# Two neighbouring rows per partition for the expert down weights, and a Silu that writes even and odd columns apart

## The chip, the cores and the metric

The kernel runs on one core of a Trainium2 chip. A core has TensorE (matrix multiplication; in the profile PE, its weight loads PEld), VectorE (DVE), ScalarE (ACT), GpSimd (POOL) and SyncE (SP), which issues the DMAs, and 16 DMA engines that move data between device memory and the on-chip memory SBUF. Matmuls write to PSUM. The metric is device time in microseconds (us); less is better.

## The reference

A trunk of two decoder layers, 256 tokens of width 1024, all in float32. Each layer has attention and a state-space mixer side by side, then a channel mixer: a dense SwiGLU in layer 0, and in layer 1 a mixture of eight experts of which each token takes two. Only the experts matter here:

```
def swiglu(h, w_gate, w_up, w_down):
    return (jax.nn.silu(h @ w_gate) * (h @ w_up)) @ w_down

logits = (hf @ router_w).astype(jnp.float32)
top_val, top_idx = lax.top_k(logits, TOP_K)          # TOP_K = 2 of 8
gates = jax.nn.softmax(top_val, axis=-1)
# per expert e: rows of its tokens -> swiglu(x, w_gate[e], w_up[e], w_down[e]) * gate, added to the token
```

An expert has w_gate and w_up of 1024 x 3584 and w_down of 3584 x 1024. The down projection sums over the 3584 columns of silu(gate) * up: in which order they are summed is free, as long as a column of the product meets its own row of w_down.

## The kernel before, in words

**Weights as a stream.** All weights pass once through SBUF as units of 1 MB, [128 partitions x 2048 floats]. `Stream` keeps their order: SyncE issues the load of a unit as soon as a buffer is free (eight `raw` buffers, and `slot` buffers lent by other tiles when those are done; line 124 is the DMA). A `slot` can be two or four smaller tiles; such a load is issued in pieces.

**Two kinds of experts.** The experts are taken in an order found at run time and alternate between two kinds, "H" and "L". An H expert has up to 128 token rows. Its weights are split in two parts that TensorE multiplies fast, `hi` (ScalarE, L157) and `lo` (VectorE, L158), two halves of 1024 floats per unit, and each product takes three matmuls (L698, L699, L700; L699 is the one that needs `lo`). An L expert has 64 rows and is multiplied in plain float32 from the raw tile (gate and up L1524, down L1546), both halves of TensorE's columns at once.

**Chunks.** Each expert goes through its 3584 columns in chunks of 1024, 1024, 1024 and 512. For a chunk the kernel makes gate (`g`) and up (`u`) in PSUM, then Silu of `g` to SBUF on ScalarE (L1672) and the product with `u` on VectorE (L1673), both named `sg`, 128 x 512 each: an H chunk of 1024 columns has two, an H chunk of 512 or an L chunk one (the L form of the last chunk has 256 columns per half). Then `sg` is transposed in blocks of 128 columns (L1575 for H, L1533 for L), and the transposed blocks are multiplied with the down weights into `ps_d` and `ps_a` (H) or `ps_m` (L). A down unit is 256 rows of w_down, two blocks of 128 rows, one for each of two neighbouring transposed blocks. Chunks of an H and an L expert take turns, and the down matmuls of a chunk run after gate and up of the next.

**What sets the order.** The order on each engine is fixed when the program is built, by a scheduler that follows the program's data; on the chip each engine works through its list and waits for semaphores. VectorE's list has `sg` products and `lo` splits in one row, ScalarE's has Silus and `hi` splits.

The change touches `add_m` (lines 344 to 353), which describes the loads of expert weights, and the loop of the expert stage in `moe` (lines 1659 to 1675). In `add_m` the source of a unit is

```
.rearrange("(k p) f -> p k f", p=P)
```

so that partition p gets row p of each block of 128 rows: two pieces of 4 KB, 512 KB apart in device memory, for a down unit.

Of the kernel before, what the change touches and what calls it, by code (L numbers as in the profile page):

```python
# [11 lines left out]
AF = mybir.ActivationFunctionType  # L12
OP = mybir.AluOpType
AX = mybir.AxisListType

P = 128
# [203 lines left out]
def trunk(ctx, tc, x, c, positions, ada_w, ada_b, norm_mix_g, norm_ffn_g, w_in, w_out, attn_sinks,  # L220
# [3 lines left out]
    V, A, G, PE = nc.vector, nc.scalar, nc.gpsimd, nc.tensor  # L224
# [7 lines left out]
    def ps(tag):  # L232
        return psum.tile([P, 512], F32, name="ps_" + tag, tag=tag, bufs={"w": 3, "m": 3, "d": 1, "a": 1}[tag])
# [110 lines left out]
    def add_m(tag, w4d, p, r0, rows, c0, width):  # L344
        def loads():
            e = expert_at[p]
            if isinstance(e, int):
                src = w4d[0, e, r0:r0 + rows, c0:c0 + width].rearrange("(k p) f -> p k f", p=P)
            else:
                src = w4d[0, bass.ds(e, 1), r0:r0 + rows, c0:c0 + width].rearrange("e (k p) f -> p (e k) f", p=P)  # L350
            return [(0, 2048, src)]

        units.append(dict(kind="w" if kinds[p] == "H" else "m", tag=(tag, p), loads=loads, n=2048))
# [12 lines left out]
    for p, ch in items:  # L366
# [4 lines left out]
        rows = 2048 // width * P  # L371
# [60 lines left out]
    p = ps("w")  # L432
# [29 lines left out]
    for b in range(2):  # L462
        for h in range(2):
            p = ps("w")
# [896 lines left out]
    def moe(route):  # L1361
# [20 lines left out]
        for b in range(2):  # L1382
            V.max_index(ix[:, b, :], mx[:, b, :], lo8[:, b, :])
        V.tensor_tensor(oh8, iota8[:, None, None, :].to_broadcast([P, 2, 2, NE]), ix[:, :, 0:2, None].to_broadcast([P, 2, 2, NE]),
                        op=OP.is_equal)
# [52 lines left out]
        wide = act.tile([P, 4, NE, NE], F32, name="sort", tag="sq", bufs=3)  # L1438
# [66 lines left out]
        def gather(ps_, oh):  # L1505
            return [lambda k2=k2: gather_part(ps_, oh, k2) for k2 in range(4)] + [lambda: info(ps_, oh)]
# [5 lines left out]
        def step_pend():  # L1512
            if pend:
                pend.pop(0)()
# [14 lines left out]
        def transpl(sg, width):  # L1529
            nm = width // 2 // P  # L1530
            p_ = ps("m")
            for m_ in range(nm):
                PE.transpose(p_[:, m_ * P:(m_ + 1) * P], sg[:, m_ * P:(m_ + 1) * P], ident)  # L1533
            ht = act.tile([P, nm, 2, half], F32, name="ht", tag="mt", bufs=2)
            A.activation(ht.rearrange("p m c s -> p (m c s)"), p_[:, 0:nm * P], AF.Copy)
            return ht

        def downl(p, ch, y, ht):
            c0, width = chunks[ch]
            nm = width // 2 // P  # L1540
            for u in range(width // 256):
                j = S.take_m(("d", p))
                for t_ in range(2):
                    ft = u * 2 + t_
                    for c_ in range(2):
                        PE.matmul(y[half * c_:half * (c_ + 1), :], ht[:, ft % nm, ft // nm, :],  # L1546
                                  S.col(j, t_ * D + c_ * 512, t_ * D + (c_ + 1) * 512), start=(ch == 0 and ft == 0),
                                  stop=(c0 + (ft + 1) * P == ED), skip_group_check=True)
                S.release(j)
# [20 lines left out]
        def transp(sgs):  # L1570
            out_ = []
            for sg in sgs:
                p_ = ps("m")
                for j in range(4):
                    PE.transpose(p_[:, j * P:(j + 1) * P], sg[:, j * P:(j + 1) * P], ident)  # L1575
                hh = act.tile([P, 4, P], F32R, name="hh", tag="mt", bufs=2)
                hl = act.tile([P, 4, P], F32R, name="hl", tag="pt", bufs=2)
                pv = p_.rearrange("p (j s) -> p j s", j=4)
                with tc.issue_after(S.last_hi):
                    A.activation(hh, pv, AF.Copy)  # L1580
                with tc.issue_after(S.last_lo):
                    V.tensor_tensor(hl, pv, hh.bitcast(F32), op=OP.subtract)  # L1582
                out_.append((hh, hl))
            return out_

        def down(p, ch, y, hs):
            for u in range(chunks[ch][1] // 256):
                w = S.take(("d", p), 2)
                for k in range(2):
                    ft = u * 2 + k  # L1590
                    hh, hl = hs[ft // 4]
                    for n_ in range(2):
                        mm3(y[n_], hh[:, ft % 4, :], hl[:, ft % 4, :], w.hi(k, n_ * 512, (n_ + 1) * 512),
                            w.lo(k, n_ * 512, (n_ + 1) * 512), ch == 0 and ft == 0, chunks[ch][0] + (ft + 1) * P == ED)
                    S.used()

        def combine(e, y):
# [10 lines left out]
            def piece(m2):  # L1608
                p_ = ps("m")
                for k in range(2):  # L1610
                    m_ = m2 * 2 + k
                    c0 = m_ % 4 * P
                    i, rows = (m_ // 4, slice(0, P)) if kinds[e] == "H" else (0, slice(m_ // 4 * half, (m_ // 4 + 1) * half))
                    PE.matmul(p_[:, k * T:(k + 1) * T], yh[i][rows, c0:c0 + P], oht[rows], start=True, stop=False)
                    PE.matmul(p_[:, k * T:(k + 1) * T], yl[i][rows, c0:c0 + P], oht[rows], start=False, stop=True)
                for k in range(2):
                    m_ = m2 * 2 + k
                    V.scalar_tensor_tensor(xT[:, m_, :], p_[:, k * T:(k + 1) * T], mod(1, 5)[:, m_:m_ + 1], xT[:, m_, :],
                                           op0=OP.mult, op1=OP.add)
            return [lambda m2=m2: piece(m2) for m2 in range(4)]  # L1620

        def flip(t):
            sg_, p, ch = t
            if kinds[p] == "H":
                hs = transp(sg_)
                return lambda y: down(p, ch, y, hs)
            ht = transpl(sg_[0], chunks[ch][1])
            return lambda y: downl(p, ch, y[0], ht)
# [3 lines left out]
        for p, ch in items:  # L1632
            kind = kinds[p]
            width = chunks[ch][1]
            final = (p, ch) == items[-1]
            if (p, ch) == (4, 0):
                flip(prev)(y[prev[1]])
                while pend:
                    step_pend()
                pend.extend(combine(prev[1], y[prev[1]]))  # L1640
                prev = None
                while pend:
                    step_pend()
                overflow(cnt_i, late_slot, gfull, htok_h, htok_l)
                S.lend(first_moe + LATE_LIMIT, lambda: [act.tile([P, D], F32, name="slot", tag=t) for t in ("cx", "qr")])
                S.lend(first_moe + ROWS_LIMIT, lambda: [act.tile([P, 2 * D], F32, name="slot", tag="xbc")])
            if final:
                while pend:
                    step_pend()
                fin = prefinish(p, inf)  # L1650
            nb = width // 512 if kind == "H" else 1
            g = [ps("w") for _ in range(nb)]
            if kind == "H":
                proj("g", p, g, gather((0,), oh0) if (p, ch) == (0, 0) else ())
            else:
                projl("g", p, width, g[0])
            if prev is not None:
                step = flip(prev)
            u = [ps(t) for t in ("w", "m")[:nb]]
            if kind == "H":  # L1660
                proj("u", p, u)
            else:
                projl("u", p, width, u[0])
                S.prime(LOOK + 2)
            ahead = together.get((p, ch))
            if ahead:
                oh = onehot(ahead)
            wide = 512 if kind == "H" else width // 2
            sg = []
            for g_, u_ in zip(g, u):  # L1670
                s_ = act.tile([P, 512], F32, name="sg", tag="rm", bufs=2)
                A.activation(s_[:, 0:wide], g_[:, 0:wide], AF.Silu)  # L1672
                V.tensor_tensor(s_[:, 0:wide], s_[:, 0:wide], u_[:, 0:wide], op=OP.mult)  # L1673
                sg.append(s_)
            if final:
                for b in range(2):
                    xbank(1, b, fin[3])
                tail = flip((sg, p, ch))
            if ahead:
                for f in gather(ahead, oh):  # L1680
                    f()
            if prev is not None:
                step(y[prev[1]])
                if prev[2] == LAST:
                    while pend:
                        step_pend()
                    pend.extend(combine(prev[1], y[prev[1]]))
            if ch == 0:
                y[p] = (ps("d"), ps("a")) if kind == "H" else (ps("m"),)
            prev = (sg, p, ch)  # L1690
# [134 lines left out]
```

## Time and profile before

| | |
|---|---|
| median of 3 runs | 1399.41 us (1398.51 to 1399.52) |
| the profiled execution, its own time | 1397.93 us |
| its span in the profile | 1395.8 us |
| TensorE busy | 1321.7 us, 95% |
| VectorE busy | 857.9 us, 61% |
| ScalarE busy | 643.7 us, 46% |
| main DMA queue | 466.72 MB in 155616 packets |

The profile is of one execution. A row of a timeline has the start and the duration in microseconds, the engine, the line, what is written <- what is read, the shape, and in brackets the idle time of the engine before it with what ended that. Matmuls are pipelined: one that lasts 0.40 us can be followed by the next after 0.23 us. A row of waits gives the waiting engine, tile and line, what it waited for, the total in us, how often, and the longest. A busy engine is not a limit by itself, and idle time of an engine that nobody waits for costs nothing.

### The profile page before, as it was taken

To read this page: it belongs to the slowest core of one execution; us is meant where nothing else is said; L and a number is where in the kernel's file an instruction comes from. 1 tells how busy PE (TensorE), PEld (TensorE's weight loads), DVE (VectorE), ACT (ScalarE), POOL (GpSimd) and SP (SyncE) were. 2 spreads that over 40 slices of the span, in tenths; PEclk is the share of its full clock that TensorE was granted. 3 is DMA by queue.
4 is the path that set the end of the run, shared out by engine and by line. 5 is a ranking of instruction groups with operands and counts; after the bars stand their busy time and mean duration, and the time that the engine had idled before them with its cause. 6 is when DMAs were issued, how large, how long until landed. Compare 5 with 4: busy or idle time off the path is not lost. (4 is left out here: it accounts for less than half of the span.)

```text
span 1395.8 us, 20220 instructions
## 1 busy us (share of the span) xinstructions
PE 1321.7 (95%) x7642; PEld 953.8 (68%) x7642; DVE 857.9 (61%) x1297; ACT 643.7 (46%) x923; POOL 20.1 (1%) x22
## 2 busy tenths in 40 slices
PE   6999999999899979999999999987999999999996
PEld 3788699999798868666464756656557467756643
DVE  5587598778689579556254744546537348845532
ACT  3456454444465547445143543533536236744412
POOL 0020000000020010000000000000000000000000
PEclk9999999999999989999999999997999999999998
DMA  9963799999434549899999999989999999999993
GB/s 324 349 237 109 277 388 363 325 348 340 159 127 146 197 149 340 333 406 400 402 409 409 409 409 409 398 349 400 363 409 409 402 401 409 409 379 409 402 402 127
DMA packets 158214, 468.77 MB, mean 336 GB/s; under 512 B 10560, under 2 KB 39456, under 8 KB 155040
## 3 DMA queue, kind: packets, MB, share of 16 engines
q1 hardware_dynamic: 155616, 466.72, 87.8%
q8 instruction: 61, 1.00, 0.3%
q10 hardware_dynamic: 2496, 0.72, 0.2%
q14 instruction: 41, 0.34, 0.1%
HBM read 466.36 MB, written 1.05 MB: 335 GB/s over the span
## 5 line engine op out<-in xcount | busy, mean ns | idle before, releaser
L158 DVE TENSOR_TENSOR lo<-raw,hi 128x1024 fp32r<-128x1024 f32 (+1 forms) x346 | 413.4, 1226 | 98.5 <-ACT hi L157 95.3
L157 ACT ACTIVATE hi<-raw 128x1024 fp32r<-128x1024 f32 (+1 forms) x346 | 354.9, 1057 | 220.7 <-PE ps_m L699 69.2
L699 PE MATMUL ps_w<-lo,xh 128*128 128x512 f32 x352 | 141.1, 401 | 0.7 <-DVE lo L158 0.7
L700 PE MATMUL ps_w<-hi,xh 128*128 128x512 f32 x352 | 140.3, 400 | 0.2 <-DVE xh L1503 0.2
L698 PE MATMUL ps_w<-hi,xh 128*128 128x512 f32 x352 | 133.8, 404 | 6.9 <-PEq L1246 5.6
L158 DVE TENSOR_TENSOR lo<-slot,hi 128x1024 fp32r<-128x1024 f32 (+1 forms) x112 | 128.0, 1181 | 15.7 <-ACT hi L157 15.7
L157 ACT ACTIVATE hi<-slot 128x1024 fp32r<-128x1024 f32 (+1 forms) x112 | 111.6, 1026 | 33.2 <-PE ps_w L700 25.7
L1673 DVE TENSOR_TENSOR sg<-sg,ps_w 128x512 f32<-128x512 f32 (+1 forms) x32 | 20.9, 654 | 171.6 <-PE ps_w L1524 129.8
L1524 PE MATMUL ps_w<-raw,xl 128*64 128x512 f32 (+1 forms) x624 | 125.7, 545 | 0.0
L698 PE MATMUL ps_m<-act_hi,hi 128*128 128x256 f32 (+1 forms) x368 | 104.6, 285 | 7.6 <-ACT hi L157 4.7
L700 PE MATMUL ps_m<-act_hi,lo 128*128 128x256 f32 (+1 forms) x368 | 104.1, 284 | 0.4 <-DVE lo L158 0.4
L699 PE MATMUL ps_m<-act_lo,hi 128*128 128x256 f32 (+1 forms) x368 | 104.2, 284 | 0.0
L1524 PEld LDWEIGHTS ps_w<-raw,xl 128*64 128x64 f32 x624 | 43.9, 137 | 72.2 <-issue 65.7
L1580 ACT ACTIVATE hh<-ps_m 128x512 fp32r<-128x512 f32 x28 | 16.2, 595 | 154.9 <-PE ps_m L1575 131.8
L698 PEld LDWEIGHTS ps_w<-hi,xh 128*128 128x128 f32 x352 | 67.3, 192 | 23.5 <-issue 5.9
L1524 PE MATMUL ps_w<-slot,xl 128*64 128x512 f32 (+1 forms) x400 | 81.4, 536 | 0.0
L699 PEld LDWEIGHTS ps_w<-lo,xh 128*128 128x128 f32 x352 | 67.4, 191 | 17.7 <-DVE lo L158 1.9
L700 PEld LDWEIGHTS ps_w<-hi,xh 128*128 128x128 f32 x352 | 67.0, 191 | 16.4 <-DVE xh L1503 0.7
L1546 PE MATMUL ps_m<-raw,ht 128*64 128x512 f32 x328 | 76.6, 599 | 0.0
L698 PEld LDWEIGHTS ps_m<-act_hi,hi 128*128 128x128 f32 (+1 forms) x368 | 68.1, 185 | 11.5 <-ACT hi L157 5.2
L1582 DVE TENSOR_TENSOR hl<-ps_m,hh 128x512 fp32r<-128x512 f32 x28 | 18.8, 688 | 92.8 <-ACT hh L1580 92.8
L1672 ACT ACTIVATE sg<-ps_w 128x512 f32<-128x512 f32 (+1 forms) x44 | 24.9, 576 | 102.5 <-PE ps_w L1524 76.6
(428 smaller groups left out, 2484.3 us busy)
## 6 DMA issues: line engine op xcount, KB each, us to landing
raw<-in_moe_w_down SPq DMA_DIRECT2D x84, 1024.0 KB, 13.5
raw<-in_moe_w_gate SPq DMA_DIRECT2D x79, 1024.0 KB, 12.4
raw<-in_moe_w_up SPq DMA_DIRECT2D x61, 1024.0 KB, 12.6
raw<-in_ada_w SPq DMA_DIRECT2D x40, 1024.0 KB, 7.2
slot<-in_moe_w_up SPq DMA_DIRECT2D x25, 1024.0 KB, 14.0
slot<-in_moe_w_gate SPq DMA_DIRECT2D x48, 512.0 KB, 12.7
slot<-in_moe_w_up SPq DMA_DIRECT2D x46, 512.0 KB, 13.8
slot<-in_moe_w_down SPq DMA_DIRECT2D x20, 1024.0 KB, 13.7
```

Of the source, the lines that this page charges most:

```text
L157: self.last_hi = nc.scalar.activation(hi[:, o:o + w], t, AF.Copy).ins
L158: self.last_lo = nc.vector.tensor_tensor(lo[:, o:o + w], t, hi[:, o:o + w].bitcast(F32), op=OP.subtract).ins
L698: PE.matmul(o_, s_hi, m_hi, start=start, stop=False, skip_group_check=True)
L699: PE.matmul(o_, s_hi, m_lo, start=False, stop=False, skip_group_check=True)
L700: PE.matmul(o_, s_lo, m_hi, start=False, stop=stop, skip_group_check=True)
L1524: PE.matmul(b[half * c_:half * (c_ + 1), 0:wide], xl[:, kk_, :], S.col(j, o_, o_ + wide), start=(kk_ == 0), stop=(kk_ == KT - 1), skip_gro ...
L1546: PE.matmul(y[half * c_:half * (c_ + 1), :], ht[:, ft % nm, ft // nm, :], S.col(j, t_ * D + c_ * 512, t_ * D + (c_ + 1) * 512), start=(ch ...
L1580: A.activation(hh, pv, AF.Copy)
L1582: V.tensor_tensor(hl, pv, hh.bitcast(F32), op=OP.subtract)
L1672: A.activation(s_[:, 0:wide], g_[:, 0:wide], AF.Silu)
L1673: V.tensor_tensor(s_[:, 0:wide], s_[:, 0:wide], u_[:, 0:wide], op=OP.mult)
```

## The change

Three edits. A down unit's load gives each partition two neighbouring rows of w_down: partition p gets rows 2p and 2p+1 of the 256, which lie one behind the other in device memory, so that a whole-tile load has packets of 8 KB. The two matmul blocks of a unit are then its even and its odd rows. To match, Silu and the product write `sg` with the even columns of each 256 in one block of 128 and the odd in the next; they read `g` and `u` in order. `in_pairs` is the view of `sg` for that: u counts groups of 256 columns, q the pairs in it, k even or odd, and k runs fastest. The transposes, the matmuls and all other loads are the same. Loads into lent buffers of two or four small tiles keep pieces of 4 or 2 KB.

```
@@ add_m
         def loads():
             e = expert_at[p]
+            if tag == "d":
+                pick_e = w4d[0, e:e + 1] if isinstance(e, int) else w4d[0, bass.ds(e, 1)]
+                return [(0, 2048, pick_e[:, r0:r0 + rows, :].rearrange("e (p k) f -> p (e k f)", p=P))]
             if isinstance(e, int):
                 src = w4d[0, e, r0:r0 + rows, c0:c0 + width].rearrange("(k p) f -> p k f", p=P)
@@ moe
+        def in_pairs(t, w):
+            return t[:, 0:w].rearrange("p (u k q) -> p u q k", k=2, q=P)
+
...
                 s_ = act.tile([P, 512], F32, name="sg", tag="rm", bufs=2)
-                A.activation(s_[:, 0:wide], g_[:, 0:wide], AF.Silu)
-                V.tensor_tensor(s_[:, 0:wide], s_[:, 0:wide], u_[:, 0:wide], op=OP.mult)
+                sv = in_pairs(s_, wide)
+                A.activation(sv, g_[:, 0:wide].rearrange("p (u q k) -> p u q k", k=2, q=P), AF.Silu)
+                V.tensor_tensor(sv, sv, u_[:, 0:wide].rearrange("p (u q k) -> p u q k", k=2, q=P), op=OP.mult)
                 sg.append(s_)
```

## Rows read from the trace of the kernel before

**Rows 1.** The page: span, and busy time of TensorE

```profile
span 1395.8 us, 20220 instructions
...
PE 1321.7 (95%) x7642; PEld 953.8 (68%) x7642; DVE 857.9 (61%) x1297; ACT 643.7 (46%) x923; POOL 20.1 (1%) x22
```

**Rows 2.** Windows: stretch, busy us by engine, TensorE's granted clock, DMA share, GB/s

```profile
core 0: us, PE busy (x) PEld busy (x) DVE busy (x) ACT busy (x) POOL busy (x), PEclk, DMA share, GB/s
560.00:1365.00 805.00, 778.52 (x3637) 486.05 (x3635) 431.17 (x475) 354.05 (x418) 0.00 (x0) 0.99 1.01 397
...
770.00:805.00 35.00, 35.00 (x155) 25.51 (x155) 24.34 (x26) 19.85 (x22) 0.00 (x0) 1.00 1.03 409
...
1130.00:1137.00 7.00, 7.00 (x34) 3.48 (x34) 0.76 (x2) 0.00 (x0) 0.00 (x0) 1.00 1.05 387
```

**Rows 3.** Waits of TensorE in 560 to 1365 us, longest in total first

```profile
PE ps_m L1533 <- DVE sg L1673: 6.9, 8, 0.9
PE ps_w L698 <- PEq L1246: 5.6, 1, 5.6
PE ps_m L1614 <- DVE oht L1606: 4.3, 1, 4.3
PE ps_d L699 <- DVE lo L158: 2.7, 2, 1.3
PE ps_m L1614 <- ACT yh L1603: 1.6, 2, 0.8
PE ps_m L1614 <- DVE xT L1618: 1.3, 2, 0.7
```

**Rows 4.** Timelines of ScalarE, VectorE and TensorE, 1340 to 1349 us

```profile
1340.83 2.00 ACT L157 ACTIVATE hi<-slot 128x1024 fp32r<-128x1024 f32 x2 [0.84 <-DMA slot<-in_moe_w_down]
...
1346.33 0.69 DVE L1673 TENSOR_TENSOR sg<-sg,ps_w 128x512 f32<-128x512 f32 x1 [15.22 <-PE ps_w L1524]
1346.93 1.22 DVE L158 TENSOR_TENSOR lo<-slot,hi 128x1024 fp32r<-128x1024 f32 x1
...
1348.20 0.50 PE L699 MATMUL ps_d<-lo,hh 128*128 128x512 f32 x1 [1.33 <-DVE lo L158]
```

**Rows 5.** Timelines of VectorE and TensorE, 1050 to 1054 us

```profile
1051.29 0.69 DVE L1673 TENSOR_TENSOR sg<-sg,ps_w 128x512 f32<-128x512 f32 x1 [12.48 <-PE ps_w L1524]
1051.89 1.22 DVE L158 TENSOR_TENSOR lo<-slot,hi 128x1024 fp32r<-128x1024 f32 x1
...
1052.03 0.66 PE L1533 MATMUL ps_m<-ident,sg 128*128 128x128 f32 x4 [0.86 <-DVE sg L1673]
...
1053.17 0.50 PE L699 MATMUL ps_d<-lo,hh 128*128 128x512 f32 x1
```

**Rows 6.** Lines by form: count | busy us, mean ns of one | idle before

```profile
L1673 DVE TENSOR_TENSOR sg<-sg,ps_w 128x512 f32<-128x512 f32 x28 | 19.2, 687 | 158.0 <-PE ps_w L1524 123.8 <-PE ps_w L700 34.2
...
L1673 DVE TENSOR_TENSOR sg<-sg,ps_w 128x256 f32<-128x256 f32 x4 | 1.7, 421 | 13.6 <-issue 7.7 <-PE ps_w L1524 5.9
...
L1333 DVE TENSOR_REDUCE shw<-shw 128x8 f32<-128x64 f32 x1 | 0.3, 262 | 0.0
...
L1445 DVE TENSOR_REDUCE keys<-sort 128x8 f32<-128x64 f32 x1 | 0.2, 220 | 0.0
...
L1448 DVE TENSOR_REDUCE keys<-sort 128x8 f32<-128x64 f32 x1 | 0.2, 214 | 0.0
...
L1672 ACT ACTIVATE sg<-ps_w 128x512 f32<-128x512 f32 x40 | 23.4, 595 | 85.5 <-PE ps_w L1524 59.6 <-PE ps_w L700 25.5
...
L1672 ACT ACTIVATE sg<-ps_w 128x256 f32<-128x256 f32 x4 | 1.5, 384 | 17.0 <-PE ps_w L1524 17.0
```

**Rows 7.** Timelines of ScalarE, VectorE and TensorE, 1017 to 1021 us

```profile
1017.79 0.60 ACT L1672 ACTIVATE sg<-ps_w 128x512 f32<-128x512 f32 x1
1018.29 1.05 ACT L157 ACTIVATE hi<-raw 128x1024 fp32r<-128x1024 f32 x1
...
1019.37 1.23 DVE L158 TENSOR_TENSOR lo<-raw,hi 128x1024 fp32r<-128x1024 f32 x1 [3.24 <-ACT hi L157]
...
1020.86 0.39 PE L699 MATMUL ps_w<-lo,xh 128*128 128x512 f32 x1
```

**Rows 8.** DMA issues of down weights: count, KB each, median us to landing

```profile
raw<-in_moe_w_down SPq DMA_DIRECT2D x84, 1024.0 KB, 13.5
...
slot<-in_moe_w_down SPq DMA_DIRECT2D x20, 1024.0 KB, 13.7
```

## The prediction

> **What bounds the kernel now.** I read the page first. TensorE is busy for 1321.7 of 1395.8 us [rows 1], which alone settles nothing, because the expert stage (from about 560 us to 1365 us) keeps the DMA engines as busy. So I took the windows of that stage next [rows 2]. Over 805 us TensorE is busy 778.5 us, and the DMA engines show a share of 1.01 at 397 GB/s. In a typical 35 us piece both columns are full, 35.00 us of TensorE and 1.03 of DMA at 409 GB/s. Which one waits for the other has to come from the waits. The idle time of TensorE in the stage is 805.0 - 778.5 = 26.5 us, and its eleven rows of waits account for 26.3 us of it; the six largest are shown [rows 3]. The reader is to see that no row names a DMA. The largest, 6.9 us in eight pieces, is a wait for the VectorE product `sg` (L1673); 2.7 us in two pieces is a wait for `lo` (L158).
>
> Then I looked at a place where weights are late. At 1340.83 ScalarE starts its split of a down weight after waiting 0.84 us for a DMA [rows 4]. TensorE does not feel it: the second half of the split, `lo`, stands on VectorE behind `sg`, which needs the end of the up projection and runs only at 1346.33. So `lo` starts at 1346.93, over six microseconds after the DMA landed. TensorE paces the stage, transfers run at their cap a little ahead of it, and the exposed holes are the places where VectorE's `sg` is in front.
>
> **The change, part by part.** No instruction is added, removed or moved: every engine's list stands in the same order with the same count. Two things differ: the shape of 104 DMAs, and the address pattern of 44 Silus (L1672) and 44 products (L1673).
>
> *The DMAs.* 84 + 20 whole-tile down loads [rows 8] get one packet of 8 KB for two of 4 KB. At 409 GB/s over 16 engines a 4 KB packet holds its engine 16 x 4096 / 409 = 160.2 ns; in a stretch where the narrow chunk's 2 KB packets are on the wire the rate is 387 GB/s [rows 2], 84.7 ns for 2 KB. The second 2 KB of a packet cost 75.5 ns, so 9.2 ns of each packet are fixed. Two 4 KB packets (320.4 ns) become one of 311.2 ns. A 1 MB load saves 8 such pairs per engine, 74 ns, and 104 loads save 7.7 us of DMA time. That is what it would be worth on the path. I take 0: TensorE's own work covers it, as no wait of TensorE in the stage ends with a DMA [rows 3]. What the faster loads do is land a little earlier. If that cover were gone, the price is the 7.7 us.
>
> *The product `sg`.* It reads the Silu from SBUF and writes back to SBUF with the pair index innermost, so that successive elements lie 128 elements (512 bytes) apart; `u` is still read in order from PSUM. Today the 512-wide form takes 687 ns and the 256-wide 421 ns, 1.04 ns per element [rows 6]. The trace has no such write, and of reads with a far inner step one clean case: the reduction L1333 reads 64 elements at a step of 32 bytes and takes 262 ns, where L1445 and L1448 reduce 64 neighbouring elements in 220 and 214 ns [rows 6]. That is 45 ns more for 64 elements, 0.70 ns each. Applied to 512 elements it is +0.36 us. The lower end is 0, since the engine may take any address at one element a cycle; a gain I exclude, as the same elements pass. The upper end is one more cycle per element, 512 x 1.04 = +0.53 us. I take +0.36, from the nearest row.
>
> [...]
>
> How often is it exposed? Between 1050 and 1053 [rows 5] TensorE ends the up projection of a half-width expert, `sg` starts at 1051.29 and ends at 1051.98, and the transpose L1533 starts at 1052.03, after 0.86 us of idle TensorE. Nothing is between them, so what `sg` grows by, TensorE waits longer; behind `sg` on VectorE stands `lo`, ending at 1053.11, and the matmul L699 that needs it starts at 1053.17, so it shifts by the same amount. This pattern occurs 8 times (the 8 pieces of 6.9 us), and the pattern of rows 4, with L699 waiting for `lo` behind `sg`, twice. That is 10 exposed products of 512 elements: 10 x 0.36 = 3.6 us (0 to 5.3 us). The other 34 have their transposes further away, behind down matmuls or the next projection, and I take them at nothing.
>
> *The Silu.* Its reads stay in order, its writes get the same step. It takes 595 ns for 512 elements and 384 ns for 256, 0.82 ns per element [rows 6]. No row has a far-stepped ScalarE write: the bounds are 0 and one more of these, +0.42 us. In the half-width experts it runs under the up projection. In the full-width experts two Silus stand in ScalarE's queue ahead of the `hi` split for the next weights [rows 7]: the second starts at 1017.79, `hi` at 1018.29, `lo` ends at 1020.60 and the matmul that needs it starts at 1020.86, a slack of 0.26 us. Four chunks look like this, and a fifth has one Silu and hardly any slack. At the upper end the price is 4 x (0.84 - 0.26) + 0.36 = 2.7 us. I take 0, because the one row on which I price a far step is a read.
>
> **Sum.** The profiled execution took 1397.93 us, its span of 1395.8 us and 2.1 us around it. 0 for the DMAs, 0 for the Silus, +3.6 us for the products: 1401.5 us. The median of the runs is 1399.41 us, 1.5 us above that execution, so the prediction is 1403.0 us.
>
> **Rivals.** *Free address pattern.* If the engines take the pattern at full rate, nothing on the path changes: 1399.4 us, and the change costs as little as it gives. For it speaks that only one small reduction shows a price; against it, that this reduction is undisturbed and dearer by a fifth.
>
> *Transfers decide.* If the stage really runs at the pace of the loads, the 7.7 us come out: 1399.4 - 7.7 = 1391.7 us, and anything over 2.8 us of it already counts as faster. For it: a DMA share of 1.03 at a flat 409 GB/s [rows 2], and ScalarE waiting for down weights [rows 4]. Against it: 26.3 of 26.5 us of TensorE's idle time have other names. It decides from the point where loads land later than `sg` ends. [...] The rows of TensorE's waits do not show it here.
>
> *Both engines pay a full cycle per element.* 5.3 us for products and 2.7 us for Silus: 1407.4 us.
>
> *8 KB packets move worse than 4 KB ones.* If a load took 5% longer (0.13 us, 104 times), 13 us of DMA time would use up the lead that rows 4 show to be short, and I would expect some 4 us of new waits: about 1403 us, slower for another reason. Nothing in the rows speaks for it.
>
> **How the numbers follow.** A change under 0.2% (2.8 us) cannot be told from none. Forecast (products pay, Silus hidden) 0.38; both pay in full 0.12; worse packets 0.03; free pattern 0.37; transfers decide 0.10. That gives slower 0.53, same 0.37, faster 0.10. The range reaches from just under the free case to near the full price, 1398.4 to 1406.6 us; the forecast's own is 1401.5 to 1405.0.
>
> **What would show it.** L1673's successor at 512 elements should take about 1.05 us (687 ns if the pattern is free, 1.22 us at a full cycle), and TensorE's wait for it should grow from 6.9 to about 9.8 us in eight pieces, with the one for `lo` from 2.7 to 3.4 us. Silu should stay near 595 ns, or else `hi` and `lo` after it come late and L699 gets waits with full-width experts. GB/s in windows of down loads should rise from 409 towards 420 with no gain in time. The prediction is wrong if the product's duration stays put, if a wait of TensorE for a DMA disappears that I did not see, or if the expert stage shortens by microseconds.

## The result, and the profile after

The changed kernel takes 1406.17 us in the median of 6 runs (1404.38 to 1407.81), the kernel before 1398.76 us in 6 runs beside them (1398.31 to 1399.52). The ratio is 1.0051, with a 95% interval from 1.0041 to 1.0062: slower by some 7 us. The forecast of slower holds, but its price, 3.6 us, is half of what came: the time stands just inside the wide range (to 1406.6 us) and above the forecast's own (1401.5 to 1405.0 us). The profiled execution took 1406.9 us, with a span 9.0 us longer than before.

The page of the changed kernel, with the packets, bytes and share of the main DMA queue in its last row, answers to [rows 1] and to the table ahead:

```profile
span 1404.8 us, 20226 instructions
...
PE 1322.7 (94%) x7642; PEld 954.0 (68%) x7642; DVE 871.5 (62%) x1297; ACT 659.5 (47%) x923; POOL 20.1 (1%) x22
...
q1 hardware_dynamic: 142304, 466.72, 86.9%
```

TensorE does the same work (1322.7 us against 1321.7). VectorE has 13.6 us more, ScalarE 15.8. The same bytes went in 13312 fewer packets, which is 104 loads of 128 pairs made into one.

The windows of the expert stage, with the columns of [rows 2], and the DMA issues of down weights, which answer to [rows 8]:

```profile
560.00:1375.00 815.00, 783.58 (x3654) 488.57 (x3655) 444.95 (x481) 369.28 (x420) 0.00 (x0) 0.99 1.00 395
770.00:805.00 35.00, 35.00 (x152) 27.38 (x152) 28.70 (x29) 21.15 (x22) 0.00 (x0) 1.00 1.02 413
```

```profile
raw<-in_moe_w_down SPq DMA_DIRECT2D x84, 1024.0 KB, 11.7
...
slot<-in_moe_w_down SPq DMA_DIRECT2D x20, 1024.0 KB, 11.0
```

In the shorter window the rate went from 409 to 413 GB/s, and a load lands 1.8 to 2.7 us earlier after its issue. TensorE is full there as before; whether the loads matter at all is left to the first experiment.

The lines by form of the two operations (L1679 is the Silu, L1680 the product), which answer to [rows 6]:

```profile
L1679 ACT ACTIVATE sg<-ps_w 128x512 f32<-128x512 f32 x40 | 43.0, 1111 | 85.2 <-PE ps_w L1527 59.7 <-PE ps_w L703 25.5
L1680 DVE TENSOR_TENSOR sg<-sg,ps_w 128x512 f32<-128x512 f32 x28 | 30.4, 1084 | 154.8 <-PE ps_w L1527 123.4 <-PE ps_w L703 31.4
```

The product grew from 687 to 1084 ns, +0.40 us; +0.36 was forecast. The Silu grew from 595 to 1111 ns, +0.52 us, which is more than the upper bound of 0.42 that I had set.

The waits of TensorE between 560 and 1375 us, and below them those between 545 and 570 us, which answer to [rows 3]:

```profile
PE ps_m L1536 <- DVE sg L1680: 9.9, 8, 1.2
PE ps_w L701 <- PEq L1249: 5.0, 1, 5.0
PE ps_m L1617 <- DVE oht L1609: 4.3, 1, 4.3
PE ps_d L702 <- DVE lo L158: 3.3, 2, 1.6
PE ps_w L702 <- DVE lo L158: 2.5, 7, 0.7
```

```profile
PE ps_m L1497 <- DVE sg L1680: 0.7, 1, 0.7
```

One row of before from 560 to 1365 us, which [rows 3] leave out, belongs beside them:

```profile
PE ps_w L699 <- DVE lo L158: 0.7, 1, 0.7
```

The wait of the transposes for `sg` grew from 6.9 to 9.9 us in the same eight pieces, and the wait for `lo` behind `sg` from 2.7 to 3.3 us in two. Both are as forecast (9.8 and 3.4). Two waits were not forecast. In the projections TensorE waits seven times for `lo`, 2.5 us, where before it was 0.7 us once. And before the gather of the next experts (L1497) it waits 0.7 us for `sg`, once; before, no wait for `sg` stands between 545 and 570 us.

The timelines of VectorE and TensorE between 1057 and 1060 us show one of the eight places; they answer to [rows 5]:

```profile
1057.17 1.07 DVE L1680 TENSOR_TENSOR sg<-sg,ps_w 128x512 f32<-128x512 f32 x1 [12.48 <-PE ps_w L1527]
1058.09 1.20 DVE L158 TENSOR_TENSOR lo<-slot,hi 128x1024 fp32r<-128x1024 f32 x1
...
1058.30 0.66 PE L1536 MATMUL ps_m<-ident,sg 128*128 128x128 f32 x4 [1.24 <-DVE sg L1680]
...
1059.35 0.50 PE L702 MATMUL ps_d<-lo,hh 128*128 128x512 f32 x1
```

The idle time before the transposes is 1.24 us for 0.86, 0.38 us more, which is what this product grew by (1.07 us for 0.69), and the matmul on `lo` shifts along without a wait of its own. The timelines of ScalarE and VectorE between 1022 and 1028 us, and of TensorE's wait there, answer to [rows 7]:

```profile
1022.46 2.03 ACT L1679 ACTIVATE sg<-ps_w 128x512 f32<-128x512 f32 x2 [2.42 <-PE ps_w L703]
1024.28 2.01 ACT L157 ACTIVATE hi<-raw 128x1024 fp32r<-128x1024 f32 x2
...
1025.38 2.36 DVE L158 TENSOR_TENSOR lo<-raw,hi 128x1024 fp32r<-128x1024 f32 x2 [3.87 <-ACT hi L157]
...
1025.99 0.40 PE L701 MATMUL ps_m<-hi,xh 128*128 128x512 f32 x1
1026.66 0.50 PE L702 MATMUL ps_w<-lo,xh 128*128 128x512 f32 x1 [0.27 <-DVE lo L158]
```

The two Silus now take 2.03 us in front of `hi`, `lo` waits 3.87 us for `hi` (3.24 before), and TensorE, which had 0.26 us of slack here, waits 0.27 us. That is the cover whose loss the prediction priced at 2.7 us and then took at 0.

### The profile page after: what moved, and what is told of

Its sections match the earlier page's. It is cut to its first block, busy times and chain, and to the rows that moved or that the text cites. A ratio compares the mean times of both kernels' runs of the same rounds, so it can differ in the third digit from the quotient of the medians.

```text
span 1404.8 us, 20226 instructions
## 1 busy us (share of the span) xinstructions
PE 1322.7 (94%) x7642; PEld 954.0 (68%) x7642; DVE 871.5 (62%) x1297; ACT 659.5 (47%) x923; POOL 20.1 (1%) x22
## 3 DMA queue, kind: packets, MB, share of 16 engines
HBM read 466.36 MB, written 1.05 MB: 333 GB/s over the span
## 5 line engine op out<-in xcount | busy, mean ns | idle before, releaser
L1680 DVE TENSOR_TENSOR sg<-sg,ps_w 128x512 f32<-128x512 f32 (+1 forms) x32 | 32.9, 1027 | 168.4 <-PE ps_w L1527 129.3
L1679 ACT ACTIVATE sg<-ps_w 128x512 f32<-128x512 f32 (+1 forms) x44 | 45.5, 1067 | 102.2 <-PE ps_w L1527 76.6
```

The source lines that it names most:

```text
L1679: A.activation(sv, g_[:, 0:wide].rearrange("p (u q k) -> p u q k", k=2, q=P), AF.Silu)
L1680: V.tensor_tensor(sv, sv, u_[:, 0:wide].rearrange("p (u q k) -> p u q k", k=2, q=P), op=OP.mult)
```

## The experiments

The theory after the trace: the packets are worth nothing, and the whole loss is the far step in SBUF, which costs by two ways, products before transposes and Silus before the splits. The rivals: the loads pay or cost a part, or the Silus are hidden and all of it is the products. The first two kernels take the change apart; the next two match the rows without a far step in SBUF. Each kernel was run beside the kernel before, whose medians there were 1399.78 us (first four kernels), 1398.62 us and 1399.03 us (the kernel on the clock). A ratio comes from those runs, with its 95% interval in brackets, and need not be the quotient of two medians printed here.

**The packets alone.** The Silu and the product as before, the loads as changed (lines against the changed kernel, here and below unless said otherwise).

```
-                sv = in_pairs(s_, wide)
-                A.activation(sv, g_[:, 0:wide].rearrange(...), AF.Silu)
-                V.tensor_tensor(sv, sv, u_[:, 0:wide].rearrange(...), op=OP.mult)
+                A.activation(s_[:, 0:wide], g_[:, 0:wide], AF.Silu)
+                V.tensor_tensor(s_[:, 0:wide], s_[:, 0:wide], u_[:, 0:wide], op=OP.mult)
```

> The 104 down loads of 8 KB packets alone, Silu and product writing in order as before (so the hidden columns meet other weight rows than the reference's; the amount of work is the same). My theory, that TensorE paces the expert stage and the loads only run ahead of it: within 2 us of the kernel before, about 1398.5 us (0 for the packets), Silu 595 ns and product 687 ns again, a load landing some 2 us earlier than the 13.5 us of before. Rival, the transfers decide part of the stage: faster by up to the 7.7 us of DMA time, 1391 us. Rival, longer packets hurt: slower by 3 us or more with waits of TensorE on DMAs.

Measured: 1399.42 us, ratio to before 1.0001 (0.9992 to 1.0010). The DMA issues and TensorE's two first waits in this kernel:

```profile
raw<-in_moe_w_down SPq DMA_DIRECT2D x84, 1024.0 KB, 12.5
...
slot<-in_moe_w_down SPq DMA_DIRECT2D x20, 1024.0 KB, 12.0
```

```profile
PE ps_m L1536 <- DVE sg L1676: 6.9, 8, 0.9
PE ps_w L701 <- PEq L1249: 5.7, 1, 5.7
```

The loads land 1.0 to 1.7 us earlier (2 expected), and the waits of TensorE are as in [rows 3] to 0.1 us. The packets are worth nothing here, and the rivals of faster loads and of worse packets fall.

**The pattern alone.** The loads as before, Silu and product as changed.

```
-            if tag == "d":
-                pick_e = ...
-                return [(0, 2048, pick_e[:, r0:r0 + rows, :].rearrange("e (p k) f -> p (e k f)", p=P))]
```

> The 4 KB packets of before with the far-stepped writes of Silu and product (the hidden columns again meet other weight rows). My theory, that the address pattern is the whole loss: 1406 us, as the changed kernel, +7 us over before; product 1.08 us and Silu 1.11 us, TensorE's wait for sg 9.9 us in eight pieces and for lo near 5.8 us. If the 8 KB packets hid or caused a part, it shows here as over 2 us between this and the changed kernel: 1408 or more if the packets gave something back, 1403 or less if they cost something.

Measured: 1406.56 us, ratio 1.0053 (1.0039 to 1.0067). Product 1084 and Silu 1109 ns, the waits for `sg` 9.9 us and for `lo` 3.3 and 2.6 us. The pattern is the whole loss. The DMA issues of this kernel, with the packets of before:

```profile
raw<-in_moe_w_down SPq DMA_DIRECT2D x84, 1024.0 KB, 12.2
```

Here too the loads land 1.3 us earlier than before, so the earlier landing in the changed kernel is not the work of the packets alone.

**Pairs taken apart on the PSUM side.** The loops over a pair are turned, so that `g` and `u` are read at a step of two elements and `sg` is written in order.

```
+                sv = s_[:, 0:wide].rearrange("p (u k q) -> p u k q", k=2, q=P)
+                A.activation(sv, in_pairs(g_, wide), AF.Silu)
+                V.tensor_tensor(sv, sv, in_pairs(u_, wide), op=OP.mult)
...
-            return t[:, 0:w].rearrange("p (u k q) -> p u q k", k=2, q=P)
+            return t[:, 0:w].rearrange("p (u q k) -> p u k q", k=2, q=P)
```

> The changed kernel with the loops over a pair turned: Silu and product read g and u in PSUM at a step of two elements (8 bytes) and write sg in SBUF in order; the result is the reference's. If the far step in SBUF is what costs (my theory): Silu back near 595 ns, product back near 690 ns, kernel 1398 to 1400 us. Rival, any step costs, in PSUM too: product and Silu stay above 1 us and the time near 1406 us.

Measured: 1399.46 us, ratio 1.0004 (0.9995 to 1.0013). Its lines by form:

```profile
L1679 ACT ACTIVATE sg<-ps_w 128x512 f32<-128x512 f32 x40 | 23.4, 595 | 85.5 <-PE ps_w L1527 59.6 <-PE ps_w L703 25.5
L1680 DVE TENSOR_TENSOR sg<-sg,ps_w 128x512 f32<-128x512 f32 x28 | 19.2, 687 | 157.9 <-PE ps_w L1527 123.8 <-PE ps_w L703 34.1
```

The same matching of rows, with the same 8 KB packets, costs nothing when SBUF is written in order and PSUM is read at a step of 8 bytes. The rival, that any step costs, falls. This kernel does not set PSUM against SBUF at the same distance: what a step of 512 bytes would cost in PSUM no run shows, and the ladder below finds a distance of 8 bytes free in SBUF too. It does not beat the kernel before either.

**Pairs taken apart by the transposes.** Silu and product in order, the loads as changed, and TensorE reads every second column (lines against the kernel before).

```
+        def every_other(sg, j):
+            return sg[:, j // 2 * 256:j // 2 * 256 + 256].rearrange("p (q k) -> p k q", k=2)[:, j % 2]
...
-                    PE.transpose(p_[:, j * P:(j + 1) * P], sg[:, j * P:(j + 1) * P], ident)
+                    PE.transpose(p_[:, j * P:(j + 1) * P], every_other(sg, j), ident)
```

> Silu and product in order as before, and the 168 transposes on TensorE read every second column of sg instead (a step of 8 bytes); the result is the reference's. If TensorE takes a step of 8 bytes at its usual 137 ns weight load and 273 ns matmul: 1398 to 1400 us, as the kernel with 8 KB packets alone. Rival: the weight loads or matmuls of the transposes grow. If by half (about 0.07 to 0.14 us each), 168 of them on the engine that paces cost 12 to 23 us: 1410 to 1421 us.

Measured: 1401.2 us, ratio 1.0013 (1.0004 to 1.0022), between the two expectations. Its lines by form, and below them those of the kernel with the packets alone:

```profile
L1578 PE MATMUL ps_m<-ident,sg 128*128 128x128 f32 x112 | 20.1, 305 | 0.0
L1578 PEld LDWEIGHTS ps_m<-ident,sg 128*128 128x128 f32 x112 | 15.6, 207 | 16.9 <-issue 16.2
```

```profile
L1578 PE MATMUL ps_m<-ident,sg 128*128 128x128 f32 x112 | 17.8, 284 | 0.0
L1578 PEld LDWEIGHTS ps_m<-ident,sg 128*128 128x128 f32 x112 | 12.3, 140 | 17.0 <-issue 16.2
```

The weight load of a transpose grew by half, from 140 to 207 ns, as the rival had it. But weight loads run beside matmuls (954.0 and 1322.7 us busy in the 1404.8 us of the changed kernel), and a matmul grew by 21 ns alone, from 284 to 305: the 168 transposes brought some 2 us, not 11.

**The Silus alone, the products alone.** In the changed kernel one of the two is put back in order.

```
-                V.tensor_tensor(sv, sv, u_[:, 0:wide].rearrange(...), op=OP.mult)
+                V.tensor_tensor(s_[:, 0:wide], s_[:, 0:wide], u_[:, 0:wide], op=OP.mult)
```

> The changed kernel with the far-stepped write in the Silu alone; the product reads and writes sg in order, so it multiplies columns that do not belong together, in the same amount of work. My theory of the trace after: Silu 1.11 us, product 687 ns; the wait for sg in eight pieces back at 6.9 us, and the Silus cost by delaying hi, and so lo, in the full-width chunks: seven waits for lo of 2 to 2.6 us in sum, kernel 2 to 3 us over before, 1401 to 1402 us. Rival, the Silus are hidden as I predicted and only the products cost: time of before, 1399 us.

```
-                A.activation(sv, g_[:, 0:wide].rearrange(...), AF.Silu)
+                A.activation(s_[:, 0:wide], g_[:, 0:wide], AF.Silu)
```

> The changed kernel with the far step in the product alone (read and write); the Silu writes in order, so the columns multiplied do not belong together. My theory: product 1.08 us, Silu 595 ns; wait for sg 9.9 us in eight pieces, lo 3.3 us in two, no seven waits for lo: 8 x 0.38 + 2 x 0.3 = 3.6 us, and up to 1.7 us more at the first full-width chunk, where the gather waits for sg and the clock was lower after it: 1402.5 to 1404.5 us. Rival, products alone make the whole loss: 1406 us. Rival, the lower clock at 560 us needs the Silus too: 1402.5 us at most.

Measured: Silus alone 1400.77 us, ratio 1.0016 (1.0007 to 1.0025); products alone 1404.06 us, ratio 1.0036 (1.0023 to 1.0050). By the ratios that is +2.2 us (1.0 to 3.5) and +5.0 us (3.2 to 7.0), and their sum, 7.2, is the loss of the pattern within its interval. The waits of TensorE with the Silus alone, then with the products alone:

```profile
PE ps_m L1536 <- DVE sg L1680: 6.9, 8, 0.9
...
PE ps_w L702 <- DVE lo L158: 2.5, 7, 0.7
```

```profile
PE ps_m L1536 <- DVE sg L1680: 9.9, 8, 1.2
...
PE ps_d L702 <- DVE lo L158: 3.3, 2, 1.6
```

Each takes its own waits and leaves the other's. The products' rows give 3.0 + 0.6 = 3.6 us, the sum of the prediction to the tenth; the rest of their 5.0 us is elsewhere, if it is more than noise.

The matmuls of an execution can be matched one by one with those of before, and the delay of each read off. In the execution with the products alone the delay grows by 0.28 to 0.31 us at each of the ten places, 3.0 us in all, and not at the Silus. In that with the Silus alone it grows by 0.35 to 0.83 us in each of seven chunks of full-width experts, 4.0 us in all, and not at the products; 1.0 us of that is gained back in one place between 946 and 966 us, of which more below. The changed kernel's execution has both, 3.0 and 4.0 us at the same places. So the rows of waits, which grow by 1.8 us for `lo` in the projections, show less than half of what the Silus take. The timeline above has the reason: the matmul at 1025.99 us lasts 0.40 us, but the next usually follows after 0.23 us. The one that waits starts 0.67 us later; the row counts 0.27 us as idle, and the delay is 0.44 us.

**One place undone: the clock.** In the changed kernel TensorE waits 0.7 us for `sg` just before 556.5 us, ahead of the second part of the gather, and the granted clock falls some microseconds later. Windows 560 to 564 us of before, of the changed kernel, and of the one with the products alone:

```profile
560.00:564.00 4.00, 4.00 (x19) 3.25 (x18) 2.21 (x2) 2.80 (x3) 0.00 (x0) 1.00 0.54 179
```

```profile
560.00:564.00 4.00, 4.00 (x15) 3.23 (x15) 1.24 (x6) 0.75 (x2) 0.00 (x0) 0.57 0.80 317
```

```profile
560.00:564.00 4.00, 4.00 (x19) 3.43 (x19) 1.24 (x6) 0.28 (x2) 0.00 (x0) 0.65 0.85 326
```

Matched matmul by matmul, the changed kernel loses 0.7 us in the hole and 1.5 us more by 564 us against before; the kernel with the pattern alone and that with the products alone lose the same 2.2 us here, and that with the Silus alone none. The next kernel keeps the far step everywhere but in chunk 1 of expert 0, whose products stand ahead of that gather.

```
+                if (p, ch) == (0, 1):
+                    sv, src = in_order(s_, wide), lambda t: psum_pairs(t, wide)
```

> The changed kernel with one of its 28 places undone: the second chunk of expert 0 writes sg in order (reading g and u in PSUM at a step of two elements), the other chunks write at the far step; the result is the reference's. My theory, that the two far-stepped products ahead of the gather make a hole of 0.7 us on TensorE at 556 us, and that the granted clock falls after it: no wait for sg before L1497, granted clock 1.00 between 560 and 564 us (0.57 in the changed kernel), and about 2 us of the 7.4 us come back: 1404 us. Rival, the lower clock does not hang on the hole: clock 0.57 to 0.8 again there, and under 1 us comes back, 1405.4 us.

Measured: 1405.76 us, ratio 1.0046 (1.0032 to 1.0059). The gather in its timeline of TensorE, and its window:

```profile
554.97 0.61 PE L1497 MATMUL ps_m<-oh,htok_l 128*128 128x128 f32 x4
555.55 0.66 PE L1497 MATMUL ps_m<-oh,htok_h 128*128 128x128 f32 x4
```

```profile
560.00:564.00 4.00, 4.00 (x19) 3.26 (x18) 2.20 (x6) 2.12 (x2) 0.00 (x0) 1.00 0.61 234
```

The hole is gone, the clock stays at 1.00 and none of the 2.2 us is lost, so in this place it went as the theory has it. Over all traces the granted clock between 560 and 564 us is 0.57 to 0.78 in the four kernels with far-stepped products in that chunk and 1.00 in the seven others. The time is the rival's, though: 0.4 us less than the changed kernel, inside both intervals. The trace says why in part. Up to 564 us this execution has regained 2.2 us on the changed kernel's, and it gives back 1.3 us between 953 and 965 us, where TensorE waits for a branch (5.6 us here, 5.0 us in the changed kernel's execution) and then does more of its work at the lower clock (from 957 to 961 us it is busy for 3.52 us here and 1.77 us there, at a granted clock of 0.50 in both). Against before, the changed kernel gains 1.3 us in that place, the pattern alone and the Silus alone 1.0 us each, and the products alone and this kernel nothing. Why it differs between executions was not settled. So the hole and the lower clock cost 2.2 us in each trace that has them, and what they are worth in the median stays open: the times cannot tell 2 us from none.

**How far is far.** Chunk by chunk the two columns of a pair stand 4, 8, 16, ... 512 bytes apart. This kernel and the next ran once each; only the durations of single rows are read from them.

```
+                q = 1 << items.index((p, ch)) % 8
+                sv = in_pairs(s_, wide, q)
```

> The changed kernel with the distance between the two columns of a pair set chunk by chunk, in eight steps: 4, 8, 16, 32, 64, 128, 256 and 512 bytes (columns meet other weight rows). [...] My theory from the trace after alone, that the price comes with the distance of neighbours in the order of access: full price at 512 bytes, 595 and 687 ns at 4 bytes, the step somewhere between. Rival, the price rises gradually with the distance.

The Silus at 8, 16, 32 and 256 bytes, from the timeline of ScalarE, and the products at 8, 16 and 256 bytes, from VectorE's:

```profile
756.96 0.60 ACT L1683 ACTIVATE sg<-ps_w 128x512 f32<-128x512 f32 x1 [6.21 <-PE ps_w L1527]
...
787.46 1.10 ACT L1683 ACTIVATE sg<-ps_w 128x512 f32<-128x512 f32 x1 [2.66 <-PE ps_w L703]
...
815.30 1.09 ACT L1683 ACTIVATE sg<-ps_w 128x512 f32<-128x512 f32 x1 [6.27 <-PE ps_w L1527]
...
899.42 1.10 ACT L1683 ACTIVATE sg<-ps_w 128x512 f32<-128x512 f32 x1 [3.11 <-PE ps_w L703]
```

```profile
763.89 0.69 DVE L1684 TENSOR_TENSOR sg<-sg,ps_w 128x512 f32<-128x512 f32 x1 [8.80 <-PE ps_w L1527]
...
799.47 1.10 DVE L1684 TENSOR_TENSOR sg<-sg,ps_w 128x512 f32<-128x512 f32 x1 [2.18 <-PE ps_w L703]
...
905.55 1.10 DVE L1684 TENSOR_TENSOR sg<-sg,ps_w 128x512 f32<-128x512 f32 x1 [1.78 <-PE ps_w L703]
```

A cliff between 8 and 16 bytes, and flat beyond (the product at 32 bytes 1.07 us, at 64 and 128 bytes the Silus 1.08 and 1.07 us, the products 1.05 us). The step of 512 bytes fell on products of 256 columns here; its price at 512 columns is that of the changed kernel. The gradual rival falls. What makes the price begin there, no run shows.

**Which side costs.** The product is formed with a constant tile, in turn all in order, with a far write, with a far read, and with both.

```
+                way = items.index((p, ch)) % 4
+                it = (in_pairs if way in (2, 3) else in_order)(iota_t, T).to_broadcast([P, wide // T, P, 2])
+                V.tensor_tensor(sv if way in (1, 3) else so, it, in_order(u_, wide), op=OP.mult)
```

> The changed kernel with the Silu in order and the product formed from u and a constant tile (it leaves the Silu out of the product), chunk by chunk in four ways: all in order, the write at the far step, the read at the far step, both. My sum took its price from a stepped read (L1333: 0.70 ns an element). If the read alone costs: 687, 687, 1084, 1084 ns in the order named (in order, write far, read far, both). If the write alone costs: 687, 1084, 687, 1084 ns. If each side costs by itself: 687, about 890, about 890, 1084 ns.

All in order, far write, far read, and both, from the timeline of VectorE:

```profile
861.94 0.69 DVE L1685 TENSOR_TENSOR sg<-iota_t,ps_w 128x512 f32<-128x512 f32 x1 [2.21 <-PE ps_w L703]
```

```profile
768.33 1.04 DVE L1685 TENSOR_TENSOR sg<-iota_t,ps_w 128x512 f32<-128x512 f32 x1 [8.80 <-PE ps_w L1527]
...
690.46 0.71 DVE L1685 TENSOR_TENSOR sg<-iota_t,ps_w 128x512 f32<-128x512 f32 x1 [12.64 <-PE ps_w L1527]
...
826.98 1.04 DVE L1685 TENSOR_TENSOR sg<-iota_t,ps_w 128x512 f32<-128x512 f32 x1 [12.48 <-PE ps_w L1527]
```

The write costs nearly everything (some 0.35 us in these rows), the read 0.02 us.

## Why the prediction was right, and where its size was off

**The packets at 0: right.** The kernel with the packets alone shows it (1.0001). The waits had said it: no row of TensorE's waits named a DMA, although the DMA share was 1.03.

**The exposed products: right in place and size.** Eight transposes and two splits behind `sg`, 3.6 us forecast, 3.6 us in the rows of waits, 3.0 us in the delay of the matmuls. But the price came from the wrong witness. I took 0.70 ns per element from a stepped read, L1333, and the experiment on the two sides shows that a far read on VectorE costs nearly nothing and the write is what costs. The cycle of the two bounds is the 1.04 ns per element read from [rows 6]; that a far step might run at today's pace was a supposition, and the product grew by 0.78 ns an element (687 to 1084 ns for 512). The agreement is chance; what makes L1333 dearer than its neighbours in [rows 6] no run here isolated.

**The other 34 products at nothing: wrong at one place.** I looked for transposes and splits behind a product, and not for who waits for the PSUM buffer that the product reads. The gather after chunk 1 of expert 0 takes its buffer from there (the row `ps_m` L1497 <- `sg`, 0.7 us). This hole of 0.7 us and the lower clock behind it take 2.2 us in the trace of the products alone; with the 3.0 us of the ten places that is 5.2 us, near the 5.0 us measured.

**The Silus at 0: the term that was mis-sized.** The slack of 0.26 us and the queue behind the Silus were read rightly, but five chunks were counted where seven lose time. The term was put at 0, with 2.7 us as its upper price; the Silus alone measured 2.2 us, and their seven chunks take 4.0 us in the trace. I chose the lower end since the only row at hand was a read on another engine. Nothing in the profile had spoken for a free write on ScalarE, and the bound of one further 0.82 ns per element was itself too low: a Silu grew by 516 ns, 1.0 ns an element.

Of the rivals, the free pattern and the deciding transfers fall, and "both pay in full" (8.0 us) was nearer to the truth than the forecast. Over 1399.41 us, which the forecast stood on, 3.6 us was forecast; over the 1398.76 us beside it the changed kernel is 7.4 us. The times of the two kernels apart would split the difference of 3.8 us into 2.2 for the Silus and 1.4 for the products, with intervals over 1 us wide to each side. The trace of the changed kernel splits its loss from 553 us on: 3.0 us at the ten products, 2.2 us at the gather, 4.0 us at the Silus and 1.3 us gained back at the branch, 7.9 us of the 8.1 us that it shows.

## What to carry to other kernels

When a layout must be permuted between two steps, see whether SBUF can be written in order and the pairs taken apart where PSUM is read: here, at a step of 8 bytes, that costs 0.0004 of the time with its interval around zero, where the write at the far step cost 0.0053. Where a trace shows that an engine waits for nothing from DMA, do not expect much of a better transfer: here it was worth nothing, at a DMA share of 1.03. Rows of waits can show less than an operation costs (1.8 of 4.0 us for the Silus here); the delay of matched matmuls shows the rest. And when an operation grows, ask for everybody who waits behind it: the next one in its own queue, the reader of its result, and whoever wants the buffer that it reads.

## What was not expected of the hardware

A Silu or product of 512 float32 elements that writes to SBUF with neighbours in order 512 bytes apart took ScalarE 1111 ns for 595 and VectorE 1084 ns for 687. From 16 to 256 bytes the price was about the same (1.07 to 1.10 us and 1.05 to 1.10 us), and at 8 bytes there was none (0.60 and 0.69 us). VectorE's read at 512 bytes cost at most 21 ns (686 to 707 ns). TensorE's weight load at a step of 8 bytes took 207 ns for 140.

Of the clock: between 556 and 560 us TensorE was busy 3.14 of 4 us in the changed kernel (3.60 before), and from 560 to 564 us the granted clock was 0.57 (1.00 before), at 4.00 us of work in both. The longer hole of 1.24 us before the transposes at 1058.30 us had no such effect: in the window from 1052 to 1066 us the granted clock is 1.00.
